# Softmax attention on one core: where the split and transposition of each rotated query stands

## Chip, core and metric

The kernel runs on one core of a Trainium2 chip. It is one inference step of a two-layer network: a gated linear attention (GLA) layer and then a grouped-query softmax attention layer. The metric is the device time of one execution in microseconds (us).

A core has five instruction queues that matter here, each worked off in order: PE (TensorE, the matmuls; PEld are its weight loads), DVE (VectorE), ACT (ScalarE), POOL (GpSimd) and SP (SyncE, which issues most DMAs). Scores and other matmul results land in PSUM, everything else lives in SBUF.

## The reference

The change touches only the softmax attention of the second layer. What has to be computed there:

```python
q, k, v, gate = split(h @ w_in)                 # 8 query heads, 2 key/value heads, head width 128
q = rms_norm(q, qn); k = rms_norm(k, kn)
qs, ks = rope_2d(qs), rope_2d(ks)               # latent tokens only
keys, vals = concat([ks, cache_k]), concat([vs, cache_v])   # 1024 + 256 keys; context tokens: 256 keys
s = einsum("bqhgd,bkhd->bhgqk", q, keys) * HEAD_DIM ** -0.5
p = softmax(s)
o = einsum("bhgqk,bkhd->bqhgd", p, vals)
out = (o * silu(gate)) @ w_out
```

There are 256 context tokens and 1024 latent tokens, a model width of 1024, and all inputs are float32.

## The kernel before

**Precision.** Every matmul operand is kept as two float16 parts, a high and a low one, whose sum stands for the float32 value. A product is three matmuls (high by high, high by low, low by high). Producing the two parts of a tile is called a split here: ACT writes the high part (`AF.Copy` with a scale), DVE writes the low part (the value less the high part).

**The steps of the attention.** `attention` goes through ten steps, `(p, c)`: `p` is one of two groups of four heads, `c` a chunk of 256 query tokens (chunk 0 is the context, with 256 keys; chunks 1 to 4 have 1280 keys). Each step has four heads, `e` = 0 to 3. For each head two blocks of 128 queries (`j` = 0, 1) are worked on by `scores`:

- PE: nine matmuls into a score tile `S` of three PSUM banks, of which there are two (three matmuls for chunk 0);
- DVE: the maximum over the keys (line 1060, tile `smx`);
- ACT: the scaled negative maximum (line 1062, `snb`), and the exponentials with their sum (line 1065, tile `p`, two buffers).

The normalisation of the exponentials is put off by one block (`put_off`, `rest`): the reciprocal of the sum and its scaled copy on DVE (lines 1081 and 1083, `srec`), the high part of the probabilities on POOL for `j` = 0 (line 1087) or on ACT for `j` = 1 (line 1089), the low part on DVE (line 1090), all into the tile `phl` with two buffers, and then a DMA transposition from SP into `PT` (line 1091). `values` later multiplies `PT` by the values (30 matmuls, 6 for chunk 0) two heads behind the scores, and `gateT` (24 matmuls) prepares the gate.

**The queries.** The queries of the next step are made during this one. For `e` = 0 and 2, `query` projects 128 tokens by four heads (24 matmuls of 512 columns), ACT copies the result to `hx`, and `queries_out(t, 0)` treats the first two heads; for `e` = 1 and 3, `query_rest` treats the other two. `queries_out` takes the sums of squares on ACT (line 878), the reciprocal root on DVE and POOL (lines 114 and 116), the rotation on POOL and DVE (lines 897, 899 and 900), and calls `split_transpose`: high part on ACT (line 925, two of 128 columns each), low part on DVE (line 926), into `xhl` with two buffers, and a DMA transposition from SP into `qT` (line 933, shown as `wst<-xhl`, since `qT` lies in a buffer called `wst`). Context queries go through lines 886, 928 and 929 instead.

**What sets the order.** The order of calls in the Python text is not the order of the instructions. The framework's scheduler simulates the program and chooses, for every engine, an order in which instructions stand in its queue; earlier calls have precedence. `with tc.issue_after(ins)` adds a rule: what the block issues on the engine of `ins` has to stand behind `ins`. `rest(last)` uses it with the score's maximum on DVE, so that the normalisation's DVE work stands behind the next maximum.

Of the kernel before, what the change touches and what calls it, by code (L numbers as in the profile page):

```python
# [52 lines left out]
class K:  # L53
# [974 lines left out]
        return i, x, self.qT[:, self.iq % 4]  # L1028


    def queries_out(self, q, j):
        i, x, qT = q
        a = slice(2 * j, 2 * j + 2)
        x = x[:, a, :]
        r = None
        if i >= NTP:
            r = self.head_rms(x)
            self.rope(x, i)
        else:
            self.head_norm(x, self.qn, x)  # L1040
        self.split_transpose(x, None, qT[:, j].rearrange("p i h t -> p (i h) t"), r)


    def scores(self, h, c, j, q, PT):
        nc = self.nc
        kv = h // (AH // KVH)
        nk = 256 if c == 0 else TS + PAST
        k0 = 10 * P if c == 0 else 0
        S = (self.S0 or self.t(self.ps, [P, 1536], F32, "S"))[:, 0:nk]
        self.S0 = None  # L1050
        qh, ql = (q[:, h % 4 // 2, m, h % 2, :] for m in range(2))
        a = 0
        while a < nk:
            n = min(512, nk - a)
            kh, kl = (t[:, kv, k0 + a : k0 + a + n] for t in (self.kTh, self.kTl))
            for m, (x, y) in enumerate(((qh, kh), (qh, kl), (ql, kh))):
                nc.tensor.matmul(S[:, a : a + n], x, y, start=m == 0, stop=m == 2)  # L1057
            a += n
        mx = self.t(self.sm, [P, 1], F32, "smx")
        last = nc.vector.tensor_reduce(mx, S, AX.X, ALU.max).ins  # L1060
        nb = self.t(self.sm, [P, 1], F32, "snb")
        nc.scalar.activation(nb, mx, AF.Copy, scale=self.nsexp)  # L1062
        p = self.t(self.sp, [P, TS + PAST], F32, "p")[:, 0:nk]
        den = self.t(self.sm, [P, 1], F32, "sden")
        nc.scalar.activation(p, S, AF.Exp, scale=self.sexp, bias=nb, accum_out=den)  # L1065
        self.rest(last)
        self.last = last
        self.put_off = p, den, PT, j, nk

# [52 lines left out]
    def query_start(self):  # L1122
        d, inv = self.ahead.pop("q0")
        lo = self.t(self.wp, [P, KT, 512], F16, "wlo0")
        self.nc.sync.dma_start(lo, d[:, 1])
        w = self.q0, lo, inv
        self.wq = [(w, [self.mulcol(self.inv_h, inv[j], self.ap, f"inv_q0{j}") for j in range(2)])]
        self.wg = [self.load_w("g0", (0, 2))]
        t = self.t(self.wst, [P, KT, 256], F32, "wst").rearrange("p k n -> p (k n)").bitcast(F16)
        self.qT = t.rearrange("p (i j m h t) -> p i j m h t", i=4, j=2, m=2, h=2)  # L1130
        self.iq = 0
        self.steps = [(p, c) for p in range(KVH) for c in ((1, 2, 3, 4, 0), OUT)[p]]
        self.todo = [(p, c, j) for p, c in self.steps for j in range(2)]
        self.q, self.half = {}, []

    def query(self):
        if self.todo:
            p, c, j = self.todo.pop(0)
            t = self.queries(2 * c + j, *self.wq[p])
            self.half.append(t)  # L1140
            self.q[(p, c, j)] = t[2]
            self.queries_out(t, 0)

    def query_rest(self):
        if self.half:
            self.queries_out(self.half.pop(), 1)

    def attention(self, wo, wk):
        self.S0, self.put_off = self.t(self.ps, [P, 1536], F32, "S"), None
        wq, wg, q, g = self.wq, self.wg, self.q, {}  # L1150
        pend, later = [], []
        t = self.t(self.sp, [P, 20, 256], F16, "PT", bufs=3)[:, 0:16, :].rearrange("p (j k) n -> p j k n", j=2)
        for j in range(2):
            self.nc.sync.dma_start(t[:, j], self.ahead["kv"][0][:, j, :, 256:512])
        wkv = [wk, (t[:, 0], t[:, 1], 256)]
        for n, (p, c) in enumerate(self.steps):
            if n == 1:
                wq.append(self.load_w("q1", 1, later))
            if n == 4:
                wg.append(self.load_w("g1", (2, 0), later))  # L1160
            if n == 6:
                wo.append(self.wload("o0", (0, 2), later))
            if n == 9:
                wo.append(self.wload("o1", 1, later))
            for e in range(4):
                h = 4 * p + e
                if later:
                    self.nc.sync.dma_start(*later.pop(0))
                PT = self.t(self.sp, [P, 20, 256], F16, "PT", bufs=3)
                self.scores(h, c, 0, q[(p, c, 0)], PT)  # L1170
                if e % 2 == 0:
                    self.query()
                    self.rest()
                    self.scores(h, c, 1, q[(p, c, 1)], PT)
                else:
                    self.query_rest()
                if len(pend) == 2:
                    self.values(*pend[0], g.pop(pend.pop(0)[0]))
                else:
                    self.key_tile(len(pend), wkv)  # L1180
                if e % 2 == 1:
                    self.scores(h, c, 1, q[(p, c, 1)], PT)
                pend.append((h, c, PT))
                if e % 2 == 1:
                    g.update({i: self.gateT(i, c, *wg[p]) for i in (h - 1, h)})
                    self.rest()
                if n == 9 and e == 0:
                    row = self.out2_load(OUT[0])
                if n == 9 and e == 1:
                    first = self.ropet.rearrange("p a b d -> p (a b d)").bitcast(F16)  # L1190
                    first = first.rearrange("p (j h t) -> p j h t", j=2, h=AH)
                    with self.tc.issue_after(self.last):
                        self.prep = self.out2_prep(row, (first[:, 0], first[:, 1]))
        self.fold_gate(*self.gate_load(1), wo[0][2] + wo[1][2])
        wo[:] = [(hi, lo, 512) for hi, lo, _ in wo]
        self.out_tile(OUT[0], 0, self.t(self.sp, [P, TS + PAST], F32, "p")[:, 0:D], wo)
        for t in pend:
            self.values(*t, g.pop(t[0]))
# [362 lines left out]
```

## Time and profile before

| | |
|---|---|
| time, median of 3 runs | 1313.71 us (1311.69 to 1316.32) |
| the profiled execution's own time | 1314.79 us |
| its span (first to last instruction) | 1313.0 us |
| granted TensorE clock, mean | 0.981 |
| busy share of the span | PE 94%, DVE 69%, ACT 54%, POOL 28% |
| attention with its queries, about 745 to 1185 us | PE busy 422.41 of 440 us, DVE 315.31, ACT 298.89, POOL 155.88 |
| after it, 1185 to 1313 us | PE busy 120.37 of 128 us |

A row of the timeline has the start in us, the length in us, the engine, the line, the operation, the output and inputs, the number of instructions merged into the row, and in square brackets the idle time of the engine just before it with what ended that time. A row of the waits has the waiting engine and line, what it waited for, and the sum, the number and the longest of these waits. The windows give the busy time of each engine in a stretch, the granted clock of PE as a share of full speed, the share of DMA engines in use, and GB/s. SPq is the queue that issues DMAs. Matmul ends are modelled, so a group's length is best read from start to start.

### The profile page before, as it was taken

The page shows a single profiled execution, that of the slowest core. Times are in us where ns is not written, and L with a number is a line of the kernel's source. Part 1 is how long each engine was busy: PE and PEld are TensorE (multiplying, and loading weights), DVE is VectorE, ACT ScalarE, POOL GpSimd, SP SyncE. Part 2 cuts the span into 40 slices and gives each one's busy share as a digit, 9 for nine tenths or more (in the row PEclk, how much of TensorE's full clock was granted, in tenths as well). Part 3 has the DMA queues.
Part 4 walks back from the last instruction along what each step waited for, and adds up shares of the span by engine and source line. Part 5 has one row for each costly group of instructions (what it writes and reads, how often), then busy time and mean ns, then how long its engine had stood idle before and what let it go on. Part 6 is the DMA issues. An engine that isn't in the chain of part 4 may idle for free. (4 is left out here: it accounts for less than half of the span.)

```text
span 1313.0 us, 22508 instructions
## 1 busy us (share of the span) xinstructions
PE 1232.5 (94%) x8058; PEld 801.3 (61%) x8058; DVE 906.1 (69%) x2110; ACT 712.2 (54%) x1730; POOL 367.4 (28%) x625
## 2 busy tenths in 40 slices
PE   4899999999989999898999898999999999989998
PEld 2366666555646556565877475766775767756444
DVE  5576868877777888655754667777767677786642
ACT  3674646565556556532433465676766677673110
POOL 1132223223322233311322534333233344322000
PEclk9999999999999999898999898999999999999999
DMA  9612655554646434258553277577948648869342
GB/s 362 245 33 77 190 171 183 173 157 126 188 133 204 143 123 141 81 130 276 132 134 121 75 171 132 119 141 140 194 96 184 147 85 151 183 133 236 127 151 80
DMA packets 335791, 199.11 MB, mean 152 GB/s; under 512 B 229838, under 2 KB 320446, under 8 KB 333376
## 3 DMA queue, kind: packets, MB, share of 16 engines
q1 hardware_dynamic: 328512, 180.79, 52.8%
q0 software_dynamic: 3728, 11.55, 2.5%
q10 hardware_dynamic: 3440, 5.35, 1.1%
q8 instruction: 63, 1.03, 0.3%
q14 instruction: 48, 0.39, 0.1%
HBM read 104.31 MB, written 37.24 MB: 108 GB/s over the span
## 5 line engine op out<-in xcount | busy, mean ns | idle before, releaser
L125 PEld LDWEIGHTS <-hT_hi 128*128 128x128 f16 x1920 | 189.8, 99 | 128.7 <-issue 15.3
L125 PE MATMUL mm<-whi,hT_hi 128*128 128x512 f16 (+1 forms) x576 | 201.7, 350 | 1.9 <-ACT gx L522 1.5
L125 PE MATMUL mm<-wlo,hT_hi 128*128 128x512 f16 (+1 forms) x576 | 201.6, 350 | 0.0
L125 PE MATMUL mm<-whi,hT_lo 128*128 128x512 f16 (+1 forms) x576 | 201.4, 350 | 0.0
L1090 DVE SCALAR_TENSOR_TENSOR phl<-p,srec,phl 128x1280 f16<-128x1280 f32 (+1 forms) x80 | 107.5, 1348 | 74.5 <-POOL phl L1087 43.9
L125 PEld LDWEIGHTS <-whi 128*128 128x128 f16 x1232 | 120.3, 98 | 59.8 <-issue 1.4
L125 PE MATMUL mm<-hT_hi,whi 128*128 128x256 f16 (+1 forms) x480 | 141.1, 294 | 0.0
L125 PE MATMUL mm<-hT_hi,wlo 128*128 128x256 f16 (+1 forms) x480 | 141.1, 294 | 0.0
L125 PE MATMUL mm<-hT_lo,whi 128*128 128x256 f16 (+1 forms) x480 | 141.1, 294 | 0.0
L1057 PE MATMUL S<-kT,wst 128*128 128x512 f16 (+1 forms) x624 | 125.3, 345 | 9.1 <-ACT p L1065 9.1
L125 PEld LDWEIGHTS <-hT_lo 128*128 128x128 f16 x960 | 94.9, 99 | 62.3 <-issue 2.2
L125 PE MATMUL mm<-PT,vh 128*128 128x256 f16 x672 | 115.0, 277 | 9.0 <-DMA PT<-phl 6.6
L1087 POOL TENSOR_SCALAR phl<-p,srec 128x1280 f16<-128x1280 f32 (+1 forms) x40 | 57.1, 1426 | 197.1 <-DVE srec L1081 71.7
L1060 DVE TENSOR_REDUCE smx<-S 128x1 f32<-128x1280 f32 (+1 forms) x80 | 101.5, 1269 | 10.3 <-PE S L1057 10.3
L1065 ACT ACTIVATE p<-S,snb,sexp 128x1280 f32<-128x1280 f32 (+1 forms) x80 | 99.3, 1242 | 8.9 <-DVE phl L1090 4.4
L1057 PEld LDWEIGHTS <-wst 128*128 128x128 f16 x624 | 61.8, 99 | 64.0 <-issue 13.6
L125 PE MATMUL mm<-PT,vl 128*128 128x256 f16 x336 | 92.9, 276 | 0.0
L148 DVE TENSOR_REDUCE wmx<-wst 128x1 f32<-128x512 f32 x104 | 64.9, 677 | 21.7 <-DMA wst<-in_gla_w_in 9.7
L125 PEld LDWEIGHTS <-wlo 128*128 128x128 f16 x616 | 60.1, 98 | 31.4 <-DVE wlo L1218 2.0
L125 PEld LDWEIGHTS <-vh 128*128 128x128 f16 x672 | 66.0, 99 | 20.0 <-issue 9.0
L1062 ACT ACTIVATE snb<-smx,nsexp 128x1 f32<-128x1 f32 x80 | 23.3, 291 | 82.7 <-DVE smx L1060 82.4
L897 POOL TENSOR_TENSOR rope<-hx,ropet 128x64 f32<-128x64 f32 x160 | 62.1, 418 | 19.8 <-ACT hx L1023 12.2
(359 smaller groups left out, 2740.7 us busy)
## 6 DMA issues: line engine op xcount, KB each, us to landing
wada<-in_w_ada SPq DMA_DIRECT2D x16, 1024.0 KB
wst<-in_gla_w_in SPq DMA_DIRECT2D x12, 1024.0 KB
wst<-in_att_w_in SPq DMA_DIRECT2D x10, 1024.0 KB
og_d<-gx SPq DMA_DIRECT2D x40, 128.0 KB
og_d<-og POOLq DMA_DIRECT2D x40, 128.0 KB, 2.8
wst<-og_d SPq DMA_DIRECT2D x5, 1024.0 KB
xr<-x_d SPq DMA_DIRECT2D x9, 512.0 KB
out<-xr ACTq DMA_DIRECT2D x17, 256.0 KB
```

The costliest lines, as they stand in the source:

```text
L125: self.nc.tensor.matmul(out, a, b, start=k == 0 and j == 0, stop=k == n - 1 and j == 2)
L148: nc.vector.tensor_reduce(mx[:, j : j + 1], st[:, 2 * j : 2 * j + 2, :], AX.XY, ALU.max, apply_absolute_value=True)
L897: nc.gpsimd.tensor_tensor(tv[:, h, :, w, :], xv[:, h, :, 1 - w, :], sn[:, :, w, :], ALU.mult)
L1057: nc.tensor.matmul(S[:, a : a + n], x, y, start=m == 0, stop=m == 2)
L1060: last = nc.vector.tensor_reduce(mx, S, AX.X, ALU.max).ins
L1062: nc.scalar.activation(nb, mx, AF.Copy, scale=self.nsexp)
L1065: nc.scalar.activation(p, S, AF.Exp, scale=self.sexp, bias=nb, accum_out=den)
L1087: nc.gpsimd.tensor_scalar(hi, p, r, 2.0 ** 14, ALU.mult, ALU.mult)
L1090: nc.vector.scalar_tensor_tensor(lo, p, r2, hi, ALU.mult, ALU.subtract)
```

## The change

`queries_out` no longer splits at once. It appends the arguments of the split to a list `splits`, and does the split itself only where its new argument `off` is false. A new function `query_split` works the list off. `scores` calls it at its end, after `rest`, with the score's maximum on DVE as the instruction to stand behind. The two calls inside `attention` pass `True`; the queries made before `attention` are split at once as before.

```diff
-    def queries_out(self, q, j):
+    def queries_out(self, q, j, off=False):
...
-        self.split_transpose(x, None, qT[:, j].rearrange("p i h t -> p (i h) t"), r)
+        self.splits.append((x, None, qT[:, j].rearrange("p i h t -> p (i h) t"), r))
+        if not off:
+            self.query_split()
+
+    def query_split(self, after=None):
+        if after is not None:
+            with self.tc.issue_after(after):
+                return self.query_split()
+        while self.splits:
+            self.split_transpose(*self.splits.pop(0))
...
         self.rest(last)
+        self.query_split(last)
         self.last = last
...
-        self.q, self.half = {}, []
+        self.q, self.half, self.splits = {}, [], []
...
-    def query(self):
+    def query(self, off=False):
...
-            self.queries_out(t, 0)
+            self.queries_out(t, 0, off)
...
-    def query_rest(self):
+    def query_rest(self, off=False):
         if self.half:
-            self.queries_out(self.half.pop(), 1)
+            self.queries_out(self.half.pop(), 1, off)
...
                 if e % 2 == 0:
-                    self.query()
+                    self.query(True)
                     self.rest()
                     self.scores(h, c, 1, q[(p, c, 1)], PT)
                 else:
-                    self.query_rest()
+                    self.query_rest(True)
```

No instruction is added or taken away; 36 splits (nine steps of four; the tenth makes no queries) are called later in the program: per split two high parts on ACT, two low parts on DVE, and one DMA transposition on SP (for context queries one of each).

## The prediction, made before the changed kernel ran

> **What bounds the kernel now.** I read the page first, then the windows around the attention, the waits of PE there, and the timeline at each place where PE waits.
>
> ```profile
> span 1313.0 us, 22508 instructions
> PE 1232.5 (94%) x8058; PEld 801.3 (61%) x8058; DVE 906.1 (69%) x2110; ACT 712.2 (54%) x1730; POOL 367.4 (28%) x625
> ...
> 745.00:1185.00 440.00, 422.41 (x2986) 293.77 (x2986) 315.31 (x623) 298.89 (x729) 155.88 (x238) 0.98 0.70 143
> 780.00:800.00 20.00, 16.09 (x94) 9.97 (x92) 13.93 (x26) 11.91 (x30) 9.77 (x13) 0.83 0.61 113
> ...
> PE S L1057 <- ACT p L1065: 9.1, 7, 3.9
> PE mm L125 <- DMA PT<-phl: 6.6, 5, 2.0
> PE mm L125 <- ACT snb L1062: 1.8, 1, 1.8
> ```
>
> PE is the bound: in the 440 us of the attention it idles 440 - 422.41 = 17.6 us. Nearly all of that is two waits: scores wait until an exponential has emptied a score tile (9.1 us), and values wait until the transposed probabilities have landed (6.6 us, and very likely the 1.8 us that the view puts down to an ACT instruction). DVE and ACT work that the change moves is worth time only where it shortens or lengthens these waits. The windows' row 780:800 has a granted clock of 0.83: there a wait also cost clock.
>
> ```profile
> 787.55 1.79 PE L1057 MATMUL S<-kT,wst 128*128 128x512 f16 x9
> 793.25 3.36 PE L1057 MATMUL S<-kT,wst 128*128 128x512 f16 x9 [3.91 <-ACT p L1065]
> ...
> 883.23 1.79 PE L1057 MATMUL S<-kT,wst 128*128 128x512 f16 x9
> 906.69 1.79 PE L1057 MATMUL S<-kT,wst 128*128 128x512 f16 x9
> 913.99 0.38 PE L125 MATMUL mm<-PT,vh 128*128 128x256 f16 x2 [0.61 <-DMA PT<-phl]
> 1015.38 0.38 PE L125 MATMUL mm<-PT,vh 128*128 128x256 f16 x2 [1.79 <-ACT snb L1062]
> 1141.05 1.78 PE L1057 MATMUL S<-kT,wst 128*128 128x512 f16 x9 [0.35 <-ACT p L1065]
> 1152.26 1.78 PE L1057 MATMUL S<-kT,wst 128*128 128x512 f16 x9 [2.57 <-ACT p L1065]
> 1157.63 1.78 PE L1057 MATMUL S<-kT,wst 128*128 128x512 f16 x9 [0.31 <-ACT p L1065]
> 1160.72 1.46 PE L1057 MATMUL S<-kT,wst 128*128 128x512 f16 x6 [1.30 <-ACT p L1065]
> ```
>
> Between 800 and 1141 us most groups follow without a gap: a half step (four scores, one query projection, two values, two gates) has a period of 906.69 - 883.23 = 23.46 us, all PE. The largest wait is at 793.25; the scores behind it took 3.36 us instead of 1.79, so it costs 3.91 + 1.57 = 5.5 us, and the values next on the slow clock somewhat more.
>
> **Part 1: the first wait (793.25).** Its causes in order:
>
> ```profile
> 775.52 1.55 DVE L1090 SCALAR_TENSOR_TENSOR phl<-p,srec,phl 128x1280 f16<-128x1280 f32 x1 [1.35 <-POOL phl L1087]
> 776.30 1.22 SPq L933 DMA_TRANSPOSE wst<-xhl  x1
> 777.62 3.14 SPq L1091 DMA_TRANSPOSE PT<-phl  x1
> 784.74 1.32 POOL L1087 TENSOR_SCALAR phl<-p,srec 128x1280 f16<-128x1280 f32 x1 [4.79 <-DMA PT<-phl]
> 786.10 3.13 DVE L1090 SCALAR_TENSOR_TENSOR phl<-p,srec,phl 128x1280 f16<-128x1280 f32 x2 [4.12 <-POOL phl L1087]
> 789.61 0.28 DVE L114 TENSOR_SCALAR hrsa<-hssq 128x2 f32<-128x2 f32 x1
> 789.80 1.48 DVE L1060 TENSOR_REDUCE smx<-S 128x1 f32<-128x1280 f32 x1
> ```
>
> The maximum at 789.80 stands behind two low parts of probabilities (3.13 us), these behind POOL, and POOL behind the transposition issued at 777.62, which must empty its `phl` buffer. No part of a query is in that chain except the transposition of 1.22 us ahead on SP. In the order of the changed kernel's instructions it stands two transpositions later, so the one of `PT` can go when its low part ends, 775.52 + 1.55 = 777.07, not 777.62: 0.55 us. The small `hrsa` (0.28) also moves behind the maximum. Together -0.8 us. Bounds: the whole wait goes (-5.5), or the split, which now stands ahead of an exponential on ACT there, passes its 0.68 us (row below, 891.93) on (+0.7). I take -0.8, since the chain ends in the POOL and DMA rows, not in the query's.
>
> **Part 2: the regular half steps.**
>
> ```profile
> 888.69 1.48 DVE L1060 TENSOR_REDUCE smx<-S 128x1 f32<-128x1280 f32 x1
> 891.93 0.68 ACT L925 ACTIVATE xhl<-hx,hrs 128x128 f16<-128x128 f32 x2
> 893.64 1.48 DVE L1060 TENSOR_REDUCE smx<-S 128x1 f32<-128x1280 f32 x1
> 893.79 0.69 ACT L925 ACTIVATE xhl<-hx,hrs 128x128 f16<-128x128 f32 x2 [1.18 <-issue]
> 895.48 1.42 ACT L1065 ACTIVATE p<-S,snb,sexp 128x1280 f32<-128x1280 f32 x1
> 896.89 1.35 ACT L1089 ACTIVATE phl<-p,srec 128x1280 f16<-128x1280 f32 x1
> 899.74 1.49 DVE L1060 TENSOR_REDUCE smx<-S 128x1 f32<-128x1280 f32 x1
> 899.85 15.68 SPq L1091 DMA_TRANSPOSE PT<-phl  x4
> 905.20 1.35 ACT L1089 ACTIVATE phl<-p,srec 128x1280 f16<-128x1280 f32 x1
> 910.88 1.55 DVE L1090 SCALAR_TENSOR_TENSOR phl<-p,srec,phl 128x1280 f16<-128x1280 f32 x1 [1.49 <-POOL phl L1087]
> 912.41 1.49 DVE L1060 TENSOR_REDUCE smx<-S 128x1 f32<-128x1280 f32 x1
> ```
>
> The first maximum of a half step (888.69, next 912.41) closes a loop over ACT, DVE, SP and POOL: maximum, exponential, second maximum, high part (896.89), transposition (899.85), 5.35 us until its buffer is refilled (905.20), exponential, high part on POOL, low part (910.88), maximum. It takes 912.41 - 888.69 = 23.72 us against 23.46 of PE: the loop is as tight as PE and slips 0.26 us per half step. That is where the waits at 913.99 and 1141.05 come from. The change acts on this loop in two ways, by two orders that the scheduler chose:
> - In nine half steps ACT's high part now stands ahead of the second exponential (1.42 us), so the transposition of 899.85 is about 1.4 us earlier and the values behind it find their `PT` sooner: the 0.61 at 913.99 and part of the 1.79 at 1015.38 can go; I take -1.0 of 2.4. But there the fourth maximum stands behind one more low part (1.55 us), and of this, after the 1.4 us gained, I reckon that some 0.6 us reach the next first maximum.
> - In the others (split behind the second exponential, maximum of the third scores ahead of the low part) the split's 0.69 us on ACT comes before the high part, and the second maximum 0.6 us sooner, since one rotation and one low part no longer stand ahead of it: nothing is left.
>
> The scores that wait for the first exponential then lose 0.6 us where they already have no slack, as at 1141.05, and in about one half step more: +1.2. Part 2: +0.2, between -2.4 (waits gone, no slip) and +5.4 (0.6 in each of the nine). On SP the moved transpositions stand behind those of `PT`, and `qT` is read half a step later, so their lateness costs nothing; if that cover went, scores would wait the 1.22 us of an issue and the landing.
>
> **Part 3: steps of chunk 0.** The scheduler puts one short score ahead of a query projection there. It may wait half a microsecond for its score tile; the next values wait for `PT` anyway. Zero, between -0.5 and +1.
>
> **Part 4: the last step.** No queries, but it takes over the lateness of the step before.
>
> ```profile
> 1148.69 1.48 DVE L1060 TENSOR_REDUCE smx<-S 128x1 f32<-128x1280 f32 x1
> 1150.72 1.40 ACT L1065 ACTIVATE p<-S,snb,sexp 128x1280 f32<-128x1280 f32 x1
> 1154.15 1.35 ACT L1089 ACTIVATE phl<-p,srec 128x1280 f16<-128x1280 f32 x1
> 1156.08 1.42 ACT L1065 ACTIVATE p<-S,snb,sexp 128x1280 f32<-128x1280 f32 x1
> ```
>
> The maximum at 1148.69 now stands ahead of a low part and is some 3 us earlier; its exponential still has to wait for that low part to free a `p` buffer, so it gains about 1.2 us, and the wait at 1152.26 shrinks from 2.57 to 1.3. It is given back at 1157.63: that score needs the exponential at 1156.08, which stands behind the high part at 1154.15, which waits for a transposition that is no earlier. At 1160.72 half of the 1.30 goes, as the maximum behind it is moved ahead. Net -0.6, between -3.9 (2.57 + 1.30) and +0.7.
>
> **The sum.** -0.8 + 0.2 + 0 - 0.6 = -1.2 us. The profiled execution took 1314.79 us for its span of 1313.0 and would take 1313.6; it lies 1.1 above the median of the three runs (1313.71), so the median becomes 1312.5. The runs before spread over 4.6 us; 0.3%, 3.9 us, is about what a measurement of this kernel can tell from no change.
>
> **Rivals.**
> *Faster: the first wait no longer slows the clock.* At 1152.26 a wait of 2.57 us left the scores at 1.78 us; 3.91 us made them 3.36. With 3.1 us, and Part 2's waits gone, the time falls by 0.8 + 1.57 + 2.4 and Part 4's better end 3.9: -8.7, hence 1305. For it: the order of the maxima. Against it: the POOL wait at 784.74, which the change moves by half a microsecond only. The Trainium skill ("TensorE: Matmul & The Clock Gate", Part 1) says that the clock halves after an idle window of about 3.4 us that runs freely; by that rule a wait cut to 3.1 us keeps full clock in some runs, and the two rows here agree with it.
>
> *Slower: the loop decides.* If the fourth maximum behind one more low part costs 0.6 us in each of the nine half steps with that order, and one of the longer waits slows the clock once more (1.57), the time rises by 5.4 + 1.6 = 7.0 to 1321. It decides from the point where the loop (23.72) exceeds PE's 23.46, which it already does. For it: two `phl` and two `p` buffers, refilled no sooner than a transposition lands. Against it: the waits of this kind before are only 0.61 and 0.35 over 14 half steps.
>
> *Nothing moves.* The splits were already behind the maxima that matter (891.93 lies behind 888.69), so the time stays at 1313.7. It lies within the forecast's 0.3%.
>
> **How the numbers follow.** Forecast with the last rival 0.42, faster 0.27, slower 0.31. Range 1306 to 1321 us: it reaches to the two outer cases and leaves out some 2 in 10. The likeliest case alone: 1310 to 1317.
>
> **What would show it.** Right: the first wait near 793 at 3 to 3.5 us; PE's waits for `p` and `PT` together within 3 us of 17.5; the fourth maximum of many half steps behind a low part; `wst<-xhl` issues behind `PT<-phl` on SP with no score waiting for `wst`. Wrong: a full clock at 780:800 (faster), or repeated waits of PE on `p` from 850 us on (slower). What would break it most is a wait that I have not seen, at a place where the scheduler changed the order of PE.

## The result and the profile after

| | before | after |
|---|---|---|
| median of 20 runs each | 1316.06 us (1310.71 to 1318.73) | 1318.09 us (1312.46 to 1322.88) |
| the profiled execution's own time | 1314.79 us | 1320.13 us |
| ratio of after to before | | 1.0027, 95% interval 1.0014 to 1.0039 |

The change made the kernel slower by 0.27% (1.0027 of 1316 us is 3.5 us more, between 1.8 and 5.1; the two medians alone stand 2.0 us apart, inside this interval, and the text goes by the ratio). I had forecast 1.2 us less. The time lies inside the range given and just inside the 0.3% that I called hard to tell from no change, but the interval lies wholly on the other side of the forecast. The two profiled executions stand 5.3 us apart, so these profiles show more of the loss than the mean run has.

The page of the changed kernel (lines 1057, 1060, 1062, 1065, 1087, 1089, 1090 and 1091 of before are 1066, 1069, 1071, 1074, 1097, 1099, 1100 and 1101 here):

```profile
span 1318.2 us, 22497 instructions
PE 1231.2 (93%) x8058; PEld 801.0 (61%) x8058; DVE 909.1 (69%) x2110; ACT 715.1 (54%) x1730; POOL 364.7 (28%) x625
```

Its windows:

```profile
780.00:800.00 20.00, 17.02 (x125) 11.98 (x124) 16.51 (x29) 13.27 (x31) 10.38 (x14) 1.00 0.67 124
800.00:1000.00 200.00, 196.07 (x1406) 137.25 (x1405) 142.01 (x281) 140.19 (x341) 64.49 (x102) 1.00 0.71 141
1000.00:1060.00 60.00, 55.05 (x381) 39.17 (x380) 36.60 (x90) 36.10 (x105) 17.93 (x34) 0.91 0.60 128
1060.00:1140.00 80.00, 77.89 (x538) 52.30 (x537) 61.88 (x114) 58.66 (x140) 34.41 (x49) 1.00 0.68 140
1140.00:1200.00 60.00, 52.94 (x397) 39.24 (x396) 48.25 (x76) 38.40 (x70) 18.23 (x25) 0.97 0.81 170
```

And its waits of PE between 745 and 1220 us:

```profile
PE mm L125 <- DMA PT<-phl: 10.1, 7, 2.0
PE mm L125 <- ACT snb L1071: 4.1, 2, 2.1
PE S L1066 <- ACT p L1074: 3.7, 4, 1.1
PE mm L125 <- ACT gx L1110: 1.6, 2, 1.0
PE mm L125 <- ACT hjunk L878: 1.5, 1, 1.5
```

The same windows of the kernel before, without 780 to 800, which stands in the prediction:

```profile
800.00:1000.00 200.00, 196.88 (x1425) 138.67 (x1423) 141.77 (x283) 137.78 (x340) 64.86 (x103) 1.00 0.70 144
1000.00:1060.00 60.00, 56.97 (x421) 40.79 (x419) 39.76 (x100) 41.54 (x117) 22.11 (x35) 1.00 0.64 133
1060.00:1140.00 80.00, 79.74 (x555) 53.78 (x553) 61.04 (x110) 56.30 (x134) 33.30 (x49) 1.00 0.72 137
1140.00:1200.00 60.00, 52.23 (x380) 37.58 (x378) 47.05 (x75) 38.12 (x71) 19.51 (x24) 0.97 0.86 185
```

A stretch loses PE time in two ways: PE idles (length less busy time), or it works at a lowered clock (length times what the granted clock lacks to 1.00, which two digits give to 0.1 us over 20 us, 0.3 over 60 and 1 over 200). Both added up, from the rows:

| stretch, us | lost before | lost after | difference |
|---|---|---|---|
| 780 to 800 | 3.9 + 3.4 = 7.3 | 3.0 + 0 = 3.0 | -4.3 |
| 800 to 1000 | 3.1 | 3.9 | +0.8 |
| 1000 to 1060 | 3.0 + 0 = 3.0 | 5.0 + 5.4 = 10.4 | +7.4 |
| 1060 to 1140 | 0.3 | 2.1 | +1.8 |
| 1140 to 1200 | 7.8 + 1.8 = 9.6 | 7.1 + 1.8 = 8.9 | -0.7 |

The differences add up to 5.0 of the 5.2 us between the two spans. So the changed kernel gains at the first scores, as it was meant to (3.4 of the 4.3 us there are clock, on which the last part has more), and gives back more, nearly all of it in 60 us in the middle. Scores wait less (9.1 to 3.7 us), values wait more (6.6 + 1.8 to 10.1 + 4.1 + 1.5 us). The wait turned from one kind into another, and the clock was lost in another place. Below, the ten steps are numbered 0 to 9 in the order of `attention`; 4 and 6 are the short ones, of chunk 0. In both profiles the scores of step 5 begin near 980 us, those of step 6 near 1025 and those of step 7 near 1060, so the loss lies in the second half of step 5 and in step 6.

### The profile page after: what moved, and what is told of

Read it like the earlier page. It is cut to its first block, busy times and chain, and to the rows that moved or that the text cites. A ratio compares the mean times of both kernels' runs of the same rounds, so it can differ in the third digit from the quotient of the medians.

```text
span 1318.2 us, 22497 instructions
## 1 busy us (share of the span) xinstructions
PE 1231.2 (93%) x8058; PEld 801.0 (61%) x8058; DVE 909.1 (69%) x2110; ACT 715.1 (54%) x1730; POOL 364.7 (28%) x625
## 5 line engine op out<-in xcount | busy, mean ns | idle before, releaser
L1100 DVE SCALAR_TENSOR_TENSOR phl<-p,srec,phl 128x1280 f16<-128x1280 f32 (+1 forms) x80 | 113.2, 1419 | 63.4 <-ACT phl L1099 33.3
L125 PE MATMUL mm<-PT,vh 128*128 128x256 f16 x672 | 118.3, 281 | 15.7 <-DMA PT<-phl 10.1
L1097 POOL TENSOR_SCALAR phl<-p,srec 128x1280 f16<-128x1280 f32 (+1 forms) x40 | 54.2, 1356 | 206.3 <-DVE srec L1091 123.8
```

Of the source, the lines that this page charges most:

```text
L125: self.nc.tensor.matmul(out, a, b, start=k == 0 and j == 0, stop=k == n - 1 and j == 2)
L1097: nc.gpsimd.tensor_scalar(hi, p, r, 2.0 ** 14, ALU.mult, ALU.mult)
L1100: nc.vector.scalar_tensor_tensor(lo, p, r2, hi, ALU.mult, ALU.subtract)
```

## The experiments

The schedule alone already tells something, without a run. With only the first halves of the queries put off (`query(True)`), every engine's instructions stand in the same order as before; with only the second halves (`query_rest(True)`) they stand as in the changed kernel. So half of the change does nothing. By steps: 4 and 6 move only two transpositions on SP, and 9 moves nothing, since it makes no queries.

### One group of steps at a time

Each kernel puts the splits off in some steps and leaves them in their old place in the others. The edit of the first; the others have `n in (1, 2)`, `n in (3, 5, 7)`, `n == 8` and `n == 5`:

```diff
-                    self.query(True)
+                    self.query(n == 0)
...
-                    self.query_rest(True)
+                    self.query_rest(n == 0)
```

> The query parts are put off in step 0 (the first attention step) alone; every other step has the instruction order of the kernel before. Theory A (the change wins at the first scores and loses it again in later steps): the traces put the lost PE time between 745 and 800 us at 9.2 us before and 5.2 us after, so this kernel is 2 to 4 us faster than before. Rival B (my prediction's size of that part, -0.8 us): within 1.5 us of before. The first wait of the scores for p is gone or under 1.5 us, instead of 3.91, by A; 3 to 3.5 us by B.

> Put off in steps 1 and 2 alone, two steps whose matmul order stays as before; only the order on ACT, DVE and SP moves. Theory A (these steps keep PE fed either way): within 1 us of before, and no wait over 0.3 us between 800 and 905 us beyond those of before. Rival B (the loop from maximum to refill decides, 0.6 us in each half step where a maximum stands behind one more low part): 1.2 to 2.4 us slower, with repeated waits for p between 810 and 905 us.

> Put off in steps 3, 5 and 7 alone: the steps in which the scheduler also moved matmuls (a score behind the values, a piece of a score behind a gate). Theory A (the loss lies here): the stretch 1000 to 1060 us lost 3.4 us before and 10.0 after, that of 1060 to 1140 us 0.6 and 2.3, so this kernel is 3 to 8 us slower than before, with values that wait 1.9 us or more for PT and run at a lowered clock behind it. Rival B (the loss is in the last step and the tail): within 1 us of before.

> Put off in step 8 alone (the last step that makes queries), whose change reaches the end of the attention and the first output tile. Theory A (its stretch 1140 to 1200 us lost 10.4 us before and 9.9 after, the tail behind it 3.1 and 4.3): within 1 us of before. Rival B (the last step and the tail carry the loss): 2 to 4 us slower, with a wait for the output factor's maximum near 1265 us.

> The splits put off in step 5 alone, the step ahead of the second short chunk. Theory A (there the low part starts 0.14 us behind a high part on GpSimd and takes 2.62 us instead of 1.55, the buffer of p is given back later, the exponential stands 2.97 us behind its maximum instead of 1.62, and in the short step scores wait 1.0 us and values 1.97 instead of 1.24): those rows stand in this run too, and it is 1 to 3.5 us slower than before. Rival B (they come from steps 3 or 7): within 1 us of before, without the rows.

| put off in steps | ratio to before | 95% interval |
|---|---|---|
| 0 | 0.9995 | 0.9978 to 1.0012 |
| 1, 2 | 1.0016 | 0.9997 to 1.0035 |
| 3, 5, 7 | 1.0029 | 1.0013 to 1.0046 |
| 8 | 0.9998 | 0.9982 to 1.0013 |
| 5 alone | 1.0034 | 1.0018 to 1.0050 |

Step 5 alone costs as much as the whole change, and more than the 1 to 3.5 us of its theory A. Steps 3, 5 and 7 came out at A's size (+3.8 us), step 8 at A's. Step 0 cost nothing that can be measured: its time is B's size, -0.7 us, though its interval (-2.9 to +1.6) reaches to A's -2 to -4, and its first wait is A's sign: the scores wait 1.43 us for `p`; but the values behind them then wait 1.88 us. Steps 1 and 2 are not settled by the time: its +2.1 us is B's size, and its interval reaches down to A's. B's waits, for `p`, are not there; but the values have one wait of 1.33 us and a projection one of 0.61 that A excludes. Their profile shows the loop at work once. Rows of the timeline of ACT and PE with steps 1 and 2 put off:

```profile
859.65 1.36 ACT L1099 ACTIVATE phl<-p,srec 128x1280 f16<-128x1280 f32 x1 [3.57 <-DMA PT<-phl]
861.59 1.42 ACT L1074 ACTIVATE p<-S,snb,sexp 128x1280 f32<-128x1280 f32 x1
...
867.61 0.38 PE L125 MATMUL mm<-PT,vh 128*128 128x256 f16 x2 [1.33 <-DMA PT<-phl]
```

ACT stands 3.57 us at a high part whose `phl` buffer a transposition still reads, with the next exponential behind it; the values then wait 1.33 us. The kernel before has no wait at either place.

**What happens in step 5.** Rows of VectorE, ScalarE, GpSimd and the DMA queue in the kernel before, at the last score of step 5:

```profile
1020.48 1.49 DVE L1060 TENSOR_REDUCE smx<-S 128x1 f32<-128x1280 f32 x1 [1.14 <-PE S L1057]
1021.89 0.15 DVE L1081 RECIPROCAL srec<-sden 128x1 f32<-128x1 f32 x1
1021.96 1.53 DVE L1090 SCALAR_TENSOR_TENSOR phl<-p,srec,phl 128x1280 f16<-128x1280 f32 x1
1022.14 2.54 POOL L1087 TENSOR_SCALAR phl<-p,srec 128x1280 f16<-128x1280 f32 x1 [1.96 <-DVE srec L1081]
1023.52 6.30 SPq L1091 DMA_TRANSPOSE PT<-phl  x2
1023.59 1.42 ACT L1065 ACTIVATE p<-S,snb,sexp 128x1280 f32<-128x1280 f32 x1
1028.62 1.36 ACT L1089 ACTIVATE phl<-p,srec 128x1280 f16<-128x1280 f32 x1 [0.27 <-DMA PT<-phl]
```

The same with step 5 put off (line numbers as in the changed kernel):

```profile
1018.98 1.49 DVE L1069 TENSOR_REDUCE smx<-S 128x1 f32<-128x1280 f32 x1 [1.14 <-PE S L1066]
1020.38 0.15 DVE L1091 RECIPROCAL srec<-sden 128x1 f32<-128x1 f32 x1
1020.46 0.40 DVE L929 TENSOR_TENSOR xhl<-hx,xhl 128x256 f16<-128x256 f32 x1
1020.64 1.42 POOL L1097 TENSOR_SCALAR phl<-p,srec 128x1280 f16<-128x1280 f32 x1 [1.96 <-DVE srec L1091]
1020.78 2.62 DVE L1100 SCALAR_TENSOR_TENSOR phl<-p,srec,phl 128x1280 f16<-128x1280 f32 x1
1023.42 12.95 SPq L1101 DMA_TRANSPOSE PT<-phl  x4
1023.43 1.42 ACT L1074 ACTIVATE p<-S,snb,sexp 128x1280 f32<-128x1280 f32 x1 [0.91 <-DVE phl L1100]
1028.97 1.36 ACT L1099 ACTIVATE phl<-p,srec 128x1280 f16<-128x1280 f32 x1 [1.10 <-DMA PT<-phl]
```

The split's low part (0.40 us, line 929) now stands between the reciprocal and the low part of `p`. Before, that low part started 0.18 us ahead of GpSimd's high part: it ran its 1.53 us and GpSimd took 2.54 instead of the 1.33 that it takes alone (row at 1086.99 below). Now GpSimd starts 0.14 us ahead, and VectorE takes 2.62 us instead of 1.53. Whoever starts second stands until the other is done. The Trainium skill ("SBUF — State Buffer", "Who interferes with whom") says this of GpSimd and of VectorE instructions that read two inputs from SBUF: they share a port that the first to start holds for its whole instruction. The rows agree nearly: GpSimd ends 1.42 - 0.14 = 1.28 us after VectorE has begun, and VectorE ends 1.34 us after that, where it takes 1.53 alone. In the 1.28 us beside GpSimd it did no more than takes it 0.2 alone.

In this execution PE is 1.5 us ahead of the one before: the last score of step 5 begins at 1017.15 us instead of 1018.65. Counted from there, the low part ends 1.41 us later than before (6.25 us behind the score instead of 4.84): 0.32 from its start, 1.09 from its length. Two things hang on its end. It is the last reader of its `p` buffer, so the exponential waits for it (0.91). And the transposition of the part goes then, at 1023.42, so the next high part waits 1.10 us for the `phl` buffer instead of 0.27. The lead of 1.5 us is gone on ACT, DVE and SP. The short step behind it has little work on PE to hide this. PE's timeline with step 5 put off:

```profile
1012.22 0.38 PE L125 MATMUL mm<-PT,vh 128*128 128x256 f16 x2 [1.99 <-ACT snb L1071]
1013.66 0.64 PE L125 MATMUL mm<-PT,vh 128*128 128x256 f16 x2
...
1034.63 0.49 PE L1066 MATMUL S<-kT,wst 128*128 128x256 f16 x3 [1.01 <-ACT p L1074]
1037.08 0.44 PE L125 MATMUL mm<-PT,vh 128*128 128x256 f16 x2 [1.96 <-DMA PT<-phl]
```

The windows behind the two waits of the values in the same run:

```profile
1012.00:1024.00 12.00, 11.79 (x87) 9.40 (x88) 8.41 (x15) 6.63 (x12) 3.41 (x5) 0.86 0.42 92
1034.00:1046.00 12.00, 9.41 (x70) 7.52 (x70) 6.64 (x23) 5.89 (x21) 4.04 (x9) 0.86 0.69 129
```

A new wait of a score (1.01), a longer one of the values (1.96 instead of 1.24), a slightly longer one ahead (1.99 instead of 1.79): 1.9 us. Behind both waits of the values the clock fell (two matmuls take 0.64 us instead of 0.38; granted 0.86 over 12 us, so 1.7 us each), where it stayed at 1.00 before. Together 5.3 us in this profile; the time says 4.5 (1.0034), between 2.4 and 6.6.

This is no accident of one execution. Eleven of the kernels here have two buffers in the old memory layout. In the five that put step 5 off, the first transposition goes 6.27 us behind the last score, a score of the short step waits 1.00 to 1.07 us and the values behind it 1.92 to 2.00; in the six others it goes 4.86 us behind, no score waits and the values wait 1.24 to 1.31. The clock fell at the second wait of the values in all five, behind the first in three of them, and at neither in the six. PE's order of instructions is the same as before up to 1043 us, behind these waits. That it is the reversed start, and not another move within step 5, which does this is read from these rows; no run reversed that alone.

### Step 7: the order on PE or the order on VectorE

In step 7 the changed schedule puts a score behind the values, and the values wait 2.07 us where nothing waited before. Its timeline with steps 3, 5 and 7 put off:

```profile
1085.93 2.35 POOL L1097 TENSOR_SCALAR phl<-p,srec 128x1280 f16<-128x1280 f32 x1 [7.31 <-DMA PT<-phl]
1088.31 1.60 DVE L1100 SCALAR_TENSOR_TENSOR phl<-p,srec,phl 128x1280 f16<-128x1280 f32 x1 [1.24 <-POOL phl L1097]
1089.84 1.48 DVE L1069 TENSOR_REDUCE smx<-S 128x1 f32<-128x1280 f32 x1
1091.68 1.42 ACT L1074 ACTIVATE p<-S,snb,sexp 128x1280 f32<-128x1280 f32 x1
1092.21 0.38 PE L125 MATMUL mm<-PT,vh 128*128 128x256 f16 x2 [2.07 <-ACT snb L1071]
```

The same place in the kernel before:

```profile
1086.80 1.48 DVE L1060 TENSOR_REDUCE smx<-S 128x1 f32<-128x1280 f32 x1
1086.99 1.33 POOL L1087 TENSOR_SCALAR phl<-p,srec 128x1280 f16<-128x1280 f32 x1 [8.56 <-DVE phl L1090]
1088.36 1.60 DVE L1090 SCALAR_TENSOR_TENSOR phl<-p,srec,phl 128x1280 f16<-128x1280 f32 x1
1088.65 1.42 ACT L1065 ACTIVATE p<-S,snb,sexp 128x1280 f32<-128x1280 f32 x1
```

Two edits to the kernel with steps 3, 5 and 7 put off. The first calls the score ahead of the values again (`lastS` is the score's last matmul; the usual call of this score is left out); the second leaves PE to the scheduler and calls the parts of `p` behind the next maximum:

```diff
+                if (n, e) == (7, 3):
+                    self.scores(h, c, 1, q[(p, c, 1)], PT)
...
+                if (n, e) == (7, 3):
+                    with self.tc.issue_after(self.lastS):
+                        self.values(*pend[0], g.pop(pend.pop(0)[0]))
```

> As the run with steps 3, 5 and 7 put off, but in the second half of step 7 the score stands ahead of the values again, as it did before. Theory A (the 2.07 us wait of the values at 1092 us is the price of the moved matmuls: the score that hid the transposition stands behind the values): that wait falls under 0.6 us and the kernel is 1.5 to 2 us faster than that run, so 1 to 2 us slower than before. Rival B (the parts on ACT and VectorE are late themselves): the wait stays or appears at the score, and the time stays 3 us above before.

```diff
-                    self.rest()
+                    if (n, e) != (7, 2):
+                        self.rest()
                     self.scores(h, c, 1, q[(p, c, 1)], PT)
```

> As the run with steps 3, 5 and 7 put off, but in the second half of step 7 the parts of the first score's exponentials are called behind the next score's maximum, so that VectorE takes the maximum ahead of the low part again (before: maximum at 1086.80 us, low part at 1088.36; with the change: it stands idle for 1.24 us for GpSimd's high part, low part at 1088.31, maximum at 1089.84, the exponential 3 us later). Theory A (that order is what costs in this step): the values' wait of 2.07 us at 1092 is under 0.6 us, and the kernel is 1.5 to 2.5 us faster than that run, 1 to 2 us slower than before. Rival B (the split itself, or the transposition behind it, is late): the wait stays over 1.5 us, the time within 1 us of that run.

With the score back in front (ratio 1.0028, 1.0016 to 1.0041) it is the score that waits, and longer (PE's timeline):

```profile
1092.63 2.72 PE L1066 MATMUL S<-kT,wst 128*128 128x512 f16 x6 [3.18 <-ACT p L1074]
```

With the maximum back in front (1.0018, 1.0003 to 1.0033) the exponential follows 1.84 us behind its maximum's start at 1087.81, the scheduler puts the score ahead of the values by itself, and of the wait only 0.27 us stay, at a score. So A of the first run falls: the order of the matmuls is a consequence. VectorE's order is the cause of the wait: it stands idle for 1.24 us for a high part of GpSimd, with a maximum behind it whose scores are ready, and the exponential starts 3.0 us later (1091.68 against 1088.65; 2.8 of it counted from the score before, which starts 0.2 later). What that is worth in time is not shown: the gain, 0.11% or 1.4 us, is in the direction of the 2.07 but not resolved. One more thing may keep it small: the wait of 2.57 us at the last step's scores (1152.26 before), which the later PE no longer has in the run with 3, 5 and 7 put off, is back with the edit (2.58).

### The whole change without step 5, and without 5 and 7

The edit is again only the condition: `n != 5`, and `n not in (5, 7)`.

> The changed kernel with the splits of step 5 alone back in their old place. Theory A (step 5 carries the loss, 1.0034 of before by itself): without it the change is between 3 us faster than before and equal to it, with the values' second wait of the short step back at about 1.2 us and no score waiting 1 us ahead of it. Rival B (the loss is spread over steps 1, 2, 5 and 7): 1 to 3 us slower than before.

> The changed kernel with the splits of steps 5 and 7 back in their old place. Theory A (step 7's wait of 2.07 us adds to step 5's): 1 to 2 us faster than the run without step 5 alone, so 1 to 5 us faster than before. Rival B (the wait of step 7 is given back later, in the last step): within 1 us of that run.

Without step 5: 0.9998 (0.9979 to 1.0017). Without 5 and 7: 0.9985 (0.9969 to 1.0002). Taking one step out of nine removes the whole loss, and taking out step 7 goes the expected way by another 0.13%, within the uncertainty. Both profiles have the values' second wait of the short step back at 1.27 to 1.31 us and no score waiting ahead of it. What remains of the change is 0.15% faster, and the interval does not tell that from no change. It still has steps 1 and 2 put off, so their +2.1 us does not show here.

### A third buffer

If the loop from one maximum to the next goes through the buffers, a third one should open it. Room for 5 kB per partition had to be made first; the control has only that (gated value in place of its gate, queries in three half tiles, fewer buffers for some columns, and smaller moves):

```diff
-        og = self.t(self.ew, [P, 256], F32, "og")
-        nc.vector.scalar_tensor_tensor(og, o, self.inv_o, g, ALU.mult, ALU.mult)
+        nc.vector.scalar_tensor_tensor(g, o, self.inv_o, g, ALU.mult, ALU.mult)
...
-        x = self.t(self.hw, [P, 4, HD], F32, "hx4")
+        x = [self.t(self.hw, [P, 2, HD], F32, "hx2", bufs=3) for _ in range(2)]
```

and then a third buffer for the parts (`phl`), as shown, or in the same way for the exponentials (`p`):

```diff
-        parts = self.t(self.sp, [P, 2 * (TS + PAST)], F16, "phl")[:, 0 : 2 * nk]
+        parts = self.t(self.sp, [P, 2 * (TS + PAST)], F16, "phl", bufs=3)[:, 0 : 2 * nk]
```

> The kernel before with its memory laid out anew to make room: the gated value is written in place of its gate, the queries lie in three half tiles, some columns have two or three buffers instead of four, the junk of the squares is half as wide. No third buffer yet. Both theories: within 2 us of before; it is the control of the next two runs.

> The control with a third buffer for the two parts of p (phl), query splits where they were before. Theory A (a part waits for the transposition that read its buffer two blocks ago, and the exponential stands behind it on ACT): the first wait (3.91 us before) and the values' waits for PT shrink, 3 to 8 us faster than before. Rival B (the loop is not what PE waits for, or the transpositions themselves are the limit): within 2 us of its control.

> The same with the query splits put off as in the changed kernel. Theory A (the loss of the changed order comes through the two buffers: a part of p starts earlier, the transpositions bunch and ACT stands behind the buffer): the loss against the other order is gone, within 1.5 us of the run with three buffers and the old place. Rival B (lateness on VectorE and the shared port): still 2 to 4 us slower than that run.

> The new memory layout with a third buffer for p (the exponentials) instead of one for its parts, the splits in their old place. Theory A (the loop that PE waits for at the first scores and near 914 to 960 us goes through the buffer of p: a score waits for an exponential, which waits until the low part two blocks ago has read p): 3 to 8 us faster than the control of the layout (1.0020 of before). Rival B (it is the buffer of the parts alone that is short): within 2 us of the control.

> The same with the splits put off everywhere. Theory A (in the changed order the exponentials stand 1.4 to 3 us longer behind their maximum because p is not free): the loss of steps 1 to 7 is gone, within 2 us of the run with three buffers of p and the old place. Rival B (the loss comes from VectorE's order, maximum behind low part): 3 us or more slower than it.

> Three buffers for the parts of p, the splits put off in all steps but step 8. Theory A (with a third buffer the place of the splits makes no difference in steps 0 to 7; the two runs stood 0.9 us apart at the attention's start and 0.9 us apart at the last score of step 8): within 1 us of the run with three buffers and the old place, 1308. Rival B (the loss is spread over the steps): 2 to 4 us slower than it.

> Three buffers, the splits put off in step 8 alone. Theory A (there the change moves the last step's values ahead of its scores, and they wait for PT: 1.57, 1.39, 1.45 and 2.86 us against 1.08 and 2.50): 3 to 5 us slower than the run with three buffers and the old place. Rival B: within 1 us of it.

> Three buffers, the splits in their old place, and the gated values of the last step written to the queries' half tiles, which are free by then, instead of in place of their gates. Theory A (the 0.2% that the new layout cost came from gates that wait in the last step for the write of the values, 2.50 us at PE): 1 to 3 us faster than the run with three buffers, 1305 to 1307, faster than both kernels. Rival B (the wait is for something else): within 1 us of it.

> Three buffers for the parts of p, the splits put off in all steps but step 8, and the gated values of the last step in the queries' half tiles. If the gains of the two runs that it joins add up (0.9922 for the one; 0.9931 against 0.9948 for the other): 0.990 to 0.992 of before, 1303 to 1306 us. If the place of the splits does nothing with three buffers: 0.993, 1307 us.

| kernel | splits | ratio to before | 95% interval |
|---|---|---|---|
| layout alone | old place | 1.0020 | 1.0006 to 1.0033 |
| third `p` | old place | 1.0006 | 0.9988 to 1.0024 |
| third `p` | put off | 0.9989 | 0.9973 to 1.0004 |
| third `phl` | old place | 0.9948 | 0.9934 to 0.9962 |
| third `phl` | put off | 0.9984 | 0.9970 to 0.9997 |
| third `phl` | put off, not in step 8 | 0.9922 | 0.9904 to 0.9940 |
| third `phl` | put off in step 8 alone | 0.9954 | 0.9936 to 0.9971 |
| third `phl`, last step's values apart | old place | 0.9931 | 0.9913 to 0.9948 |
| third `phl`, last step's values apart | put off, not in step 8 | 0.9945 | 0.9927 to 0.9964 |

PE's waits from 745 to 1200 us with the third `phl` and the old place of the splits (lines 1056 and 1064 are 1057 and 1065 of before):

```profile
PE mm L125 <- DMA PT<-phl: 7.7, 5, 2.6
PE S L1056 <- ACT p L1064: 4.9, 4, 2.2
PE mm L125 <- ACT p L1064: 1.1, 1, 1.1
```

A third buffer for the parts is worth 0.7% against its control and 0.5% against the kernel before. Of the first wait (3.91 us) 0.83 is left, at the values; with a third `p` it is still 3.20, at the score. So the loop through `phl` is what the first scores wait for, and it was open to a better remedy than moving the splits. The waits of the values for `PT`, which I had expected to shrink as well, did not (7.7 us against 6.6). The third `phl` beats both kernels, as its variants do, the one with everything put off by little. Giving the last step's values tiles of their own changed little: the wait of 2.50 us that it was aimed at is 2.57 there, and the 0.17% in time is within the intervals.

For the loss the runs say less. With a third `p` the put-off order is not slower than the old one (0.9989 against 1.0006), but the loss of step 5 is not gone: the low part of 2.62 us is still in the profile, the score's wait is gone, the values wait 2.69 us instead of 1.26, and the clock falls behind that. PE's waits over 0.3 us add up to 11.4 us against 9.9 between 760 and 1100 us (13.7 against 10.1 with two buffers), and to 5.2 against 8.0 from there to 1200: a loss and a gain that cancel. With a third `phl` and step 8 left out the put-off order is not slower either (0.9922 against 0.9948, on another chip), and up to 1100 us its waits are no longer than those of the old order (8.5 to 9.3 us in three profiles against 8.8 to 10.7 in three). That fits the thought that two buffers pass the lateness on, but does not show it: the scheduler orders PE otherwise there (a score waits 1.67 to 1.99 us near 1005, as in none of the kernels with two), so it is not the same step with one buffer more.

With everything put off and a third `phl` the kernel is slower again (0.9984 against 0.9948, on one chip; 4.7 us, more than the 2 to 4 of that run's rival). This points to step 8: behind 1100 us PE waits 7.6 and 7.8 us in the two profiles with step 8 put off and 4.4 to 5.3 in the four without. On the one chip that ran both, step 8 alone gave 0.9954, and everything but step 8 gave 0.9922. Against 0.9948, from another chip, it is not the 3 to 5 us that I expected, and the two runs that should have added up did not (0.9945). What step 8 costs with three buffers, and whether the place of the splits gains anything there, stays open; with two buffers step 8 costs nothing (0.9998).

## Why the prediction was wrong

**The bound.** Right: PE is the bound before and after, and the change acts through its waits for `p` and `PT` and the clock behind them. (Of the 6.6 us, 1.28 lie at 1186.07, behind the 440 us; inside, the waits named make 16.1 of the 17.6.)

**Part 1, the first wait: right in size, partly by luck.** I said 3 to 3.5 us and -0.8. The rows of the changed kernel:

```profile
789.10 1.78 PE L1066 MATMUL S<-kT,wst 128*128 128x512 f16 x9 [1.09 <-ACT p L1074]
792.76 0.39 PE L125 MATMUL mm<-PT,vh 128*128 128x256 f16 x2 [1.89 <-DMA PT<-phl]
```

1.09 + 1.89 = 2.98 us. Summed in this way, scores and the values behind them, the four profiles with step 0 put off and two buffers have 3.0 to 3.6 us there (mean 3.2), the seven with the old order 3.3 to 4.5 (mean 4.1). Step 0 alone measured -0.7 us (-2.9 to +1.6). The transposition does go when its low part ends, as I said. But the chain gained more than that: the `phl` buffer came free 6.2 us after the issue on the mean, instead of 7.1, and the scores' own wait fell by 2.0 us (mean 3.8 to 1.8). The values behind them then wait 1.5 us instead of 0.3, which I had not foreseen.

**Part 2, the regular half steps: +0.2, not refuted as a sum, but two of its terms were wrong.** Steps 1 and 2 measured +2.1 us (-0.4 to +4.6), and without steps 5 and 7 nothing of it shows. The wait of 1.79 at 1015.38 was to shrink; it is 1.94 to 1.99 in the five profiles with step 5 put off and 1.69 to 1.85 in the six others. And the maximum behind one more low part, which I had at 0.6 us, makes the exponential in step 7 2.8 us later: the low part's own 1.60 and the 1.24 that VectorE stands at its head, waiting for GpSimd. I had costed an instruction moved ahead by its length, and left out what it waits for itself.

**Part 3, the short steps: the step that failed.** I wrote zero, between -0.5 and +1, because the values there wait for `PT` anyway. Step 5, whose lateness the short step 6 takes over, measured +4.5 us (2.4 to 6.6), about the whole error of the forecast (1.2 + 3.5 = 4.7). The harm did not come from the matmul order that I looked at. By the rows it came from 0.40 us of a moved low part that reversed which of VectorE and GpSimd starts first. The rows for it were in the trace before: a high part on GpSimd took 2.54 us at 1022.14 and 1.33 at 1086.99. And a wait that is there anyway is not a floor: it went from 1.24 to 1.96 and took the clock with it.

**Part 4, the last step:** -0.6; step 8 alone measured -0.3 us (-2.4 to +1.7). In agreement, but by luck: the scores' waits of 2.57 and 1.30 us did not shrink by half, they turned into 0.56 at a score and 1.76 and 1.53 at values that had not waited there before.

**The rivals.** The faster one came true in its place: the clock stays at 1.00 from 780 to 800 us. I had named that as the sign of a faster kernel, and it was not, since the clock was lost again at 1012 and 1037. Nor is it a sure effect of the change: among the kernels with two buffers the clock stayed full there in three of the seven profiles with step 0 in the old order, and in three of the four with it put off. The two rows that I set side by side (2.57 us kept the clock, 3.91 lost it) were too few: waits of 2.57 and 2.58 us at the last step's scores lost it in two of six profiles. The slower rival, the loop that exceeds PE's period, is of the right kind (one place's lateness passed on through buffers), but not in the form given: not 0.6 us in nine half steps, but 4.5 in one step, and a wait of 2 us in another whose price is not resolved. My last sentence, that an unseen wait where PE's order changed would break the forecast most, was half right: in step 7 the wait came where PE's order had changed, but putting the order back did not help; in step 5 the waits came ahead of any such place.

**The other signs.** PE's waits for `p` and `PT` together were to stay within 3 us of 17.5, and did: 10.1 + 4.1 + 3.7 = 17.9, or 19.4 with the 1.5 that the view puts down to `hjunk`, a wait of the values too. The sum hid the exchange of scores for values. No score waited for `wst`, as I had said.

## What to carry to other kernels

When an instruction is put later on an engine, don't price it by its length: ask what the instruction now ahead waits for, and which neighbour on another engine loses or wins a race by it. Here a delay did harm where the step behind it is short, so cost a move step by step and look hardest at the short steps. If a loop through a double buffer is as long as the bound engine's period, another buffer is worth more than another order: here 0.5% against a loss of 0.3%.

## What the hardware showed that I had not expected

**VectorE and GpSimd exclude each other on these parts.** A low part takes 1.5 to 1.6 us alone and 2.4 to 2.6 when a high part on GpSimd started 0.1 to 0.3 us ahead; 1.8 when it started 1.06 us ahead. A high part takes 1.3 us alone and up to 2.8 when it starts second. With the put-off order VectorE loses this race more often (five low parts over 2 us, none before): its low parts are 113.2 us together instead of 107.5, GpSimd's high parts 54.2 instead of 57.1.

**A wait of 2 us can cost nearly as much again in clock, and its place decides.** In all twenty profiles of this case the granted clock is either 1.00 or 0.50. It stays at 0.50 for 3.41 us or a small multiple of that, and up to the last instructions all these stretches begin and end on one grid of 3.41 us that runs through the whole execution. Two neighbouring stretches of that grid with step 5 alone put off, then two with steps 3, 5 and 7:

```profile
1009.96:1013.37 3.41, 1.42 (x14) 1.07 (x12) 3.04 (x7) 1.95 (x4) 1.86 (x3) 1.00 1.10 205
1013.37:1016.78 3.41, 3.41 (x18) 2.44 (x17) 1.88 (x6) 2.54 (x6) 0.09 (x1) 0.50 0.61 136
...
1008.75:1012.17 3.42, 1.48 (x10) 0.73 (x9) 3.04 (x6) 0.96 (x2) 0.87 (x2) 1.00 1.08 203
1012.17:1015.58 3.41, 3.41 (x32) 2.94 (x30) 3.02 (x9) 2.54 (x5) 1.08 (x2) 1.00 0.85 178
```

In the first pair PE is idle for 1.99 us of a stretch and has half the clock in the next; in the second pair it is idle for 1.94 and keeps it. Between 760 and 1200 us of all profiles, the clock fell behind a stretch at full clock in 28 of 28 cases with more than 2.02 us idle, in 7 of 11 with 1.95 to 2.02, and in none of 2497 with less. So the wait of 1.94 to 1.99 us near 1011 cost clock in three of five profiles, according to how it lay on the grid, and the 1.69 to 1.85 of the old order never did. The two waits of the short step, with one score between them, put 2.03 to 2.74 us into one stretch in all five. The Trainium skill ("TensorE: Matmul & The Clock Gate", Part 1) ties the fall to an idle window of about 3.4 us that runs freely. The grid fits the free running; that about 2 us of idleness in a stretch are enough does not fit a whole idle window, and here the measurement decides.
